# Opening of an encoder trunk: first weights by halves, matmuls of ones, held-back second-half work, another order of early pairs

## Chip, cores and metric

One core of a Trainium2 chip. The metric is the time of one execution on the device, in microseconds; the median of the runs counts. "PE" is TensorE (matmuls), "DVE" VectorE, "ACT" ScalarE, "POOL" GpSimd, "SP" the engine that issues nearly all transfers.

## The reference

Two request groups (512 and 256 tokens, 1024 wide) pass through the same trunk. Everything is float32.

```python
def swiglu(h, wg, wu, wd):
    return (jax.nn.silu(h @ wg) * (h @ wu)) @ wd

def even_layer(x, ...):                       # layer 0
    x = x + 0.5 * swiglu(rmsnorm(x, f1_n), f1_g, f1_u, f1_d)
    x = x + mixer_ab(rmsnorm(x, mix_n), ...)  # gated mixing beside windowed attention
    x = x + 0.5 * swiglu(rmsnorm(x, f2_n), f2_g, f2_u, f2_d)
    return x

def odd_layer(x, ...):                        # layer 1
    x = x + 0.5 * swiglu(rmsnorm(x, f1_n), f1_g, f1_u, f1_d)
    x = x + mixer_c(rmsnorm(x, mix_n), ...)   # neighbourhood attention
    x = x + 0.5 * swiglu(rmsnorm(x, f2_n), f2_g, f2_u, f2_d)
    return x
```

After both layers comes a last rmsnorm. The inner width of swiglu is 2816. The change touches only the swiglu blocks and the norms ahead of them.

## The kernel before

**Phases.** Six follow one another: l0f1, l0m, l0f2, l1f1, l1m, l1f2 (swiglu blocks have an f, mixers an m). x lies in the core as eight tiles of 128 channels by 768 tokens and stays there. The tokens are worked in two halves of 384 (half 0, half 1).

**A float32 product in three.** An operand is split into a rounded part (`whi`, or a name ending in h, made on ACT) and the rest (`wlo`, or a name ending in l, made on DVE). A product of two operands takes three matmuls: high with high, high with low, low with high.

**A block by seven products.** A swiglu block works on pairs of 256 inner columns, 11 of them. Each pair's gate and up matrices are seen as 2 by 2 blocks (channels 0 to 511 and 512 to 1023, two tiles of 128 columns), as are the token halves and channel halves of x. Seven block products per matrix take the place of eight. The operands on the side of x are b11 and b21 (half 0, split directly), and t1, t2, t3, n4, b22, which need half 1; `self.made` lists those that are there. One block product is 12 matmuls of 384 columns (four channel tiles, three each).

**Early pairs.** The first four pairs (`EARLY`) begin with the two products that need half 0 only: `p1` (weights times b11, for gate and up) and `p2` (weights times b21, added into the same PSUM bank). Between them the result of `p1` is copied out (line 524), and `p2` must wait for that copy. When 1/rms of half 0 is there, `hidden(0, 0)` scales both sums and multiplies silu(gate) by up (lines 508 to 511); this frees the two banks. `ORDER` lists, by hand, the order in which the stages p1, p2 and hidden of the four early pairs are issued. Their later five products (t2, t3, n4, t1, b22) follow pair by pair. Banks come from two rings of four, `mm` and `aux`; line 481 chooses.

**1/rms beside the products.** The norm does not hold up the products: x is multiplied by its gain only, and 1/rms is applied in `hidden`. Squares are made on ACT and added on DVE (`norm_add`). `norm_tok` sums them over channels by matmuls with a column of ones and computes 1/rms in small DVE steps (`rsqrt`, lines 265 to 276), `norm_spread` makes two diagonal matrices (`diag`, DVE line 256 and ACT line 254) and spreads them over the channels by two matmuls with ones.

**Who orders what.** PE's instructions run in the order in which the program issues them. On the other engines a scheduler orders them by priority, which follows the program's order unless raised (`high_priority`); every engine then runs its own queue in order. Side work (norms, operands of half 1) lives in generators: each yields a delay, and `tick` resumes those that are due on a model clock `self.t`, which counts the matmuls issued so far (0.16 for one of 384 columns). `run_until` resumes them at once where a result is needed. So the delays (`DELAY0`, `DELAY1`: ahead of the row sum, and between it and the spread) place norm matmuls between the products in PE's queue.

**The opening.** `build` makes the constants, loads x half 0 in eight transfers with the first four weight tiles (512 KB each: gate and up of pairs 0 and 1) between them, then x half 1. `second()` makes what needs half 1 (`feed`, then squares and sums); its instructions on ACT follow the second copy of `p1` (`issue_after`).

**Other blocks.** l1f1 follows another block, so its operands of half 1 are made as the block before ends. l0f2 and l1f2 follow a mixer: `self.unfed` is not empty there, and `behind` makes the operands.

## Time and profile before

| what | us |
|---|---|
| median of 3 runs | 2620.62 |
| lowest, highest | 2618.2, 2620.9 |
| profiled execution, its own time | 2616.48 |
| its span in the profile | 2614.7 |
| PE busy in the span | 2553.1 |
| DVE busy | 2264.1 |
| ACT busy | 1366.3 |

The span is what the profiler recorded of the profiled execution; that execution's own time is 1.8 us more. The median of the other runs is 4.1 us above the profiled one. Busy shares are means over six phases and say little of one stage, so the views are read by stretches and by single rows. In a timeline row the first number is the start, the second the duration, and brackets hold the time for which the engine idled before and what ended that.

### The profile page before, as it was taken

Reading aid. Unit: us, or ns where it says so; the run is one execution under the profiler, and the core shown is the slowest. Engines: PE = TensorE matmul, PEld = TensorE weight load, DVE = VectorE, ACT = ScalarE, POOL = GpSimd, SP = SyncE. Lnnn points to the kernel's source line nnn. Section 1 sums busy time; section 2 is a strip of 40 time slices with the busy share of each in tenths; the row PEclk is TensorE's granted clock in tenths of the full one; section 3 lists DMA queues with packets and bytes.
Section 4 is the critical chain, followed back from the end, with each engine's and each line's share of the span. In section 5 each row is a group of like instructions: output and inputs, shape, how many; then the busy total and the mean of one; then the engine's idle time right before and its main releaser. Section 6 shows DMA issues by size and latency. Waiting matters only on the chain.

```text
span 2614.7 us, 41195 instructions
## 1 busy us (share of the span) xinstructions
PE 2553.1 (98%) x15094; PEld 2488.8 (95%) x15094; DVE 2264.1 (87%) x4793; ACT 1366.3 (52%) x2851; POOL 88.4 (3%) x172
## 2 busy tenths in 40 slices
PE   7999999998999999999999999999999999999997
PEld 7999999987899999999999999989898999999997
DVE  8998899889779989889999888986677699988897
ACT  7544454555655545445654445454445475444543
POOL 0000000000100000000000000001222100000000
PEclk9999999999999999999999999999999999999999
DMA  5333222421223322222322222232221332222221
GB/s 172 112 112 95 81 65 65 160 73 45 82 77 97 97 65 81 66 81 81 97 81 81 74 72 73 72 129 63 63 64 40 106 99 88 81 73 73 73 69 69
DMA packets 83898, 218.99 MB, mean 84 GB/s; under 512 B 20080, under 2 KB 32880, under 8 KB 83696
## 3 DMA queue, kind: packets, MB, share of 16 engines
q1 hardware_dynamic: 83552, 216.34, 26.3%
q8 instruction: 118, 1.93, 0.3%
q14 instruction: 84, 0.69, 0.1%
q10 hardware_dynamic: 144, 0.03, 0.0%
HBM read 206.90 MB, written 15.07 MB: 85 GB/s over the span
## 4 chain that ended last, share of the span: by engine, by line
PE 88%; DVE 8%; ACT 2%; issue 1%; DMA 1%; SPq 0%; DVEq 0%; ACTq 0%
PE ps_mm L140 55%; PE ps_aux L140 32%; DVE wlo L115 1%; PE ps_aux L144 1%; DMA raw<-in_w 1%; DVE xl L741 1%; ACT p L913 1%; DVE p L922 0%; DVE p L907 0%; DVE tl L197 0%; DVE tmp L362 0%; ACT xh L740 0%; DVE x L708 0%; DVE ol L197 0%; ACT whi L114 0%
## 5 line engine op out<-in xcount | busy, mean ns | idle before, releaser
L114 ACT CAST whi<-s 128x512 fp32r<-128x512 f32 x496 | 305.1, 620 | 413.7 <-DVE s L611 169.9
L114 ACT CAST whi<-raw 128x512 fp32r<-128x512 f32 x512 | 311.4, 618 | 232.5 <-PE ps_mm L140 98.7
L115 DVE TENSOR_TENSOR wlo<-s,whi 128x512 fp32r<-128x512 f32 x496 | 337.4, 686 | 56.3 <-ACT whi L114 53.9
L115 DVE TENSOR_TENSOR wlo<-raw,whi 128x512 fp32r<-128x512 f32 x494 | 337.7, 691 | 24.9 <-ACT whi L114 20.7
L140 PE MATMUL ps_mm<-db,whi 128*128 128x384 f32 x864 | 219.3, 334 | 0.4 <-DVE sg L508 0.4
L140 PE MATMUL ps_aux<-dt,whi 128*128 128x384 f32 x864 | 219.1, 334 | 0.0
L140 PEld LDWEIGHTS ps_mm<-db,whi 128*128 128x128 f32 x864 | 155.9, 188 | 0.7 <-DVE sg L508 0.7
L140 PEld LDWEIGHTS ps_aux<-dt,whi 128*128 128x128 f32 x864 | 156.0, 188 | 0.0
L140 PE MATMUL ps_mm<-xh,whi 128*128 128x512 f32 (+1 forms) x416 | 147.3, 354 | 3.6 <-ACT xh L740 3.6
L140 PE MATMUL ps_mm<-db,wlo 128*128 128x384 f32 x432 | 144.3, 334 | 0.0
L140 PE MATMUL ps_aux<-dt,wlo 128*128 128x384 f32 x432 | 144.3, 334 | 0.0
L140 PE MATMUL ps_mm<-xl,whi 128*128 128x512 f32 (+1 forms) x416 | 142.3, 342 | 1.1 <-DVE xl L741 1.1
L140 PE MATMUL ps_mm<-xh,wlo 128*128 128x512 f32 (+1 forms) x416 | 141.9, 341 | 0.0
L611 DVE TENSOR_TENSOR s<-raw,raw 128x512 f32<-128x512 f32 x124 | 84.0, 686 | 21.3 <-DMA raw<-in_w 21.1
L611 DVE TENSOR_TENSOR s<-raw 128x512 f32<-128x512 f32 x124 | 85.2, 687 | 18.6 <-DMA raw<-in_w 18.3
L499 DVE TENSOR_TENSOR u<-ps_aux,u 128x384 f32<-128x384 f32 x176 | 97.2, 552 | 4.0 <-PE ps_aux L140 3.9
L140 PE MATMUL ps_aux<-dh,whi 128*128 128x384 f32 x384 | 97.7, 335 | 0.6 <-DVE x L708 0.6
L913 ACT ACTIVATE p<-p,st 128x256 f32<-128x256 f32 (+3 forms) x144 | 68.9, 480 | 54.5 <-DVE st L911 54.4
L663 DVE TENSOR_TENSOR x<-ps_aux,x 128x384 f32<-128x384 f32 x160 | 84.9, 552 | 13.0 <-PE ps_aux L140 13.0
L140 PEld LDWEIGHTS ps_mm<-xh,whi 128*128 128x128 f32 x416 | 79.9, 192 | 13.9 <-ACT xh L740 4.7
L140 PE MATMUL ps_mm<-oh,whi 128*128 128x384 f32 x256 | 88.7, 346 | 4.6 <-DVE x L890 4.0
L663 DVE TENSOR_TENSOR x<-ps_mm,x 128x384 f32<-128x384 f32 x160 | 86.2, 551 | 5.8 <-PE ps_mm L140 5.4
(486 smaller groups left out, 8046.3 us busy)
## 6 DMA issues: line engine op xcount, KB each, us to landing
raw<-in_w SPq DMA_DIRECT2D x350, 512.0 KB, 3.7
xdm<-x SPq DMA_DIRECT2D x16, 384.0 KB, 2.3
x<-in_x SPq DMA_DIRECT2D x16, 192.0 KB, 5.4
x<-xdm SPq DMA_DIRECT2D x8, 384.0 KB, 3.3
xold<-xdm SPq DMA_DIRECT2D x8, 384.0 KB, 3.0
out_y<-y SPq DMA_DIRECT2D x8, 384.0 KB, 2.4
tab<-skew SPq DMA_DIRECT2D x8, 256.0 KB, 5.6
raw<-in_w SPq DMA_DIRECT2D x8, 256.0 KB, 2.6
```

Source lines behind the costliest of these rows:

```text
L114: nc.scalar.copy(hi, src)
L115: (eng or nc.gpsimd).tensor_tensor(out=lo, in0=src, in1=hi.bitcast(F32), op=ALU.subtract)
L140: self.nc.tensor.matmul(out, lhsT=lhsT, rhs=rhs, start=start, stop=stop, **kw)
L144: self.nc.tensor.transpose(out, src, self.ident)
L499: nc.vector.tensor_tensor(out=t, in0=bank[key, n], in1=t, op=ALU.add)
L611: f = lambda o, x, y, op: self.nc.vector.tensor_tensor(out=o, in0=x, in1=y, op=op)
L663: nc.vector.tensor_tensor(out=o, in0=ps, in1=o, op=ALU.add)
L741: nc.vector.scalar_tensor_tensor(out=lo, in0=src, scalar=gain, in1=hi.bitcast(F32), op0=ALU.mult, op1=ALU.subtract)
L913: nc.scalar.activation(outs[i], outs[i], AF.Exp, bias=nm[:, i : i + 1], accum_out=sm[:, i : i + 1])
```

## The change

- The first four weight tiles are loaded as eight halves of 256 KB: the channel half that `p1` needs first, then the other. The very first half goes through ACT's queue, the others through SP's, three between x's first and second four tiles and four behind those.
- The constant of ones is made before the identity; a copy on ACT of part of it stands at the start, so ACT's table load comes there.
- 22 matmuls of ones by ones (`WARM`) are issued on PE ahead of the first product. Their result is not used.
- The split of the first four weight halves is placed in ACT's queue behind the 1st, 4th, 5th and 6th square (`HOLD`).
- `second()` is held until six copies of `p1` exist and the first 1/rms has been issued; its ACT instructions follow the sixth copy, its DVE instructions the last piece of the first `diag`.
- `diag` is issued together with the row sum and `rsqrt`, and no longer at the time of the spread.
- Delays: the opening has its own for half 0 (`DELAYS`) and half 1 (`DELAYT`); `DELAY0` elsewhere goes from (7.0, 11.0) to (7.0, 13.0).
- Where no mixer precedes (l0f1 and l1f1; `mixed` is false) the early pairs go in another order, and pair 2 instead of pair 3 takes its banks from `aux`. Blocks behind mixers keep theirs.
- In the opening, b21 weights of pairs 0 and 1 lose the raised priority, and `hidden(0, 0)` of those pairs gains it.
- The transfers of the bias tables (`self.spare`) start four units later, since the eight halves count as eight units and the four tiles counted as four.

```diff
-DELAY0 = (7.0, 11.0)
+DELAY0 = (7.0, 13.0)
+DELAYS = (11.6, 8.5)
+WARM = 22
+HOLD = (0, 3, 4, 5)
 DELAY1 = (26.0, 12.0)
+DELAYT = (22.0, 12.0)
-ORDER = (0, 1, 0, 1, 0, 2, 1, 3, 2, 3, 2, 3)
+ORDERS = (0, 1, 0, 1, 2, 2, 0, 1, 3, 2, 3, 3), (0, 1, 0, 1, 0, 2, 1, 3, 2, 3, 2, 3)
...
     def norm_spread(self, y, pool=None):
 
-        nc = self.nc
+        return self.spread(self.diags(y, pool))
+
+    def spread(self, diags):
+
+        rb = self.psum(self.aux, "aux")
+        for i, diag in enumerate(diags):
+            self.mmul(rb[:, :H], self.onesr, diag, i == 0, i == 1)
+        return rb[:, :H]
...
-            self.mmul(rb[:, :H], self.onesr, diag, i == 0, i == 1)
-        return rb[:, :H]
+            res.append(diag)
+        self.rooted.append(last.ins)
+        return res
...
         with self.tc.high_priority():
-            y = self.norm_tok(self.acc, c0, c1)
+            diags = self.diags(self.norm_tok(self.acc, c0, c1))
         yield d1
         with self.tc.high_priority():
-            self.r[h] = self.norm_spread(y)
+            self.r[h] = self.spread(diags)
...
         for n in (1, 2):
-            while len(self.copied) < 2:
+            while len(self.copied) < 6 or not self.rooted:
                 yield 0.2
-            with self.tc.issue_after(self.copied[1]):
+            with self.tc.issue_after(self.copied[5]), self.tc.issue_after(self.rooted[0]):
...
-        yield from self.norm_half(h, *(DELAY1 if h else DELAY0))
+        yield from self.norm_half(h, *((DELAY1 if len(self.rooted) > 1 else DELAYT) if h else DELAY0 if self.rooted else DELAYS))
...
+        mixed = bool(self.unfed)
...
+            fresh = bool(self.first)
...
-                    mm = key == "Y" or key == "X" and p != EARLY - 1
+                    mm = key == "Y" or key == "X" and p != EARLY - (1 if mixed else 2)
...
-                with self.tc.high_priority() if early and (b in ("b11", "b21") or b == "t2" and p == EARLY - 1) else nullcontext():
+                with ExitStack() as stack:
+                    if fresh and b == "b11":
+                        stack.enter_context(self.tc.issue_after(self.squares[HOLD[len(self.copied)]]))
+                    if early and (b == "b11" or b == "b21" and not fresh or b == "t2" and p == EARLY - 1):
+                        stack.enter_context(self.tc.high_priority())
                     st = self.wsplit(w, nc.vector)
...
-                hidden(0, 0, bank["X", "gate"], bank["X", "up"])
+                with self.tc.high_priority() if fresh else nullcontext():
+                    hidden(0, 0, bank["X", "gate"], bank["X", "up"])
...
-        for p in ORDER:
+        for p in ORDERS[mixed]:
...
+            def first(i, k, eng=None):
+                name = pre + ("gate", "up")[i % 2]
+                self.raw(name, 4 * k, 4, i // 2 * 2 * P, P, raws[i][:, k * 512 : k * 512 + 512], eng)
+
+            first(0, 0, nc.scalar)
+        nc.gpsimd.memset(self.ones, 1.0)
+        nc.vector.tensor_copy(self.onesr, self.ones)
+        nc.scalar.copy(space, self.ones[:, :96])
+        make_identity(nc, self.ident)
...
+        if kind == "f":
+            ps = self.psum(self.aux, "aux")
+            for _ in range(WARM):
+                nc.tensor.matmul(ps[:, :P], lhsT=self.onesr, rhs=self.onesr, start=True, stop=True)
...
                 if h == 0 and m % 4 == 3 and kind == "f":
-                    pre = f"{self.phases[0][:2]}_ffn{self.phases[0][3]}"
-                    self.first += [self.raw(f"{pre}_w_{n}", 0, KD, m // 4 * 2 * P, P) for n in ("gate", "up")]
+                    for i in range(4):
+                        if m > 4 or i:
+                            first(i, m // 4)
```

More of the change, by code (lines that the diff above doesn't have):

```diff
@@ L97, in raw @@
         self.woff += size
-        raw = self.rawp.tile([P, nk * n], F32, tag="raw", name=f"raw{i}")
-        self.nc.sync.dma_start(raw, src)
-        if self.spare and i >= 16:
+        if raw is None:
+            raw = self.rawp.tile([P, nk * n], F32, tag="raw", name=f"raw{i}")
+        (eng or self.nc.sync).dma_start(raw, src)
+        if self.spare and i >= 20:
             self.spare.pop(0)()
@@ L1412, in build @@
         nc = self.nc
-        self.cp.tile([P, 96], F32, tag="space", name="space")
+        space = self.cp.tile([P, 96], F32, tag="space", name="space")
+        todo = [KIND[p] for p in self.phases] + [("last", 6)]
+        kind = todo[0][0]
         self.ident = self.cp.tile([P, P], F32, tag="ident", name="ident")
-        make_identity(nc, self.ident)
         self.ones = self.cp.tile([P, P], F32, tag="ones", name="ones")
-        nc.gpsimd.memset(self.ones, 1.0)
         self.onesr = self.cp.tile([P, P], F32R, tag="onesr", name="onesr")
-        nc.vector.tensor_copy(self.onesr, self.ones)
         self.gains = self.cp.tile([P, 64], F32, tag="gains", name="gains")[:, : KD * len(NORMS)]
         nc.scalar.dma_start(self.gains, self.aps["gains"])
+        if kind == "f":
+            pre = f"{self.phases[0][:2]}_ffn{self.phases[0][3]}_w_"
+            raws = [self.rawp.tile([P, KD * P], F32, tag="raw", name=f"first{i}") for i in range(4)]
+            self.first += [t.rearrange("p (k n) -> p k n", k=KD) for t in raws]
+            def first(i, k, eng=None):
[6 more added lines that the diff above has]
+        make_identity(nc, self.ident)
         self.ngains = self.cp.tile([P, 64], F32, tag="ngains", name="ngains")[:, : KD * len(NORMS)]
@@ L1424, in build @@
         self.x = [self.xp.tile([P, T], F32, tag=f"x{m}", name=f"x{m}") for m in range(KD)]
-        todo = [KIND[p] for p in self.phases] + [("last", 6)]
-        kind = todo[0][0]
         if kind == "f":
```

13 lines of the change are left out of this document (8 added, 5 removed).

## Prediction

> **What bounds the kernel now.** I read the page's head and chain first, then TensorE's waits over the span, then the opening by stretches and in order of time.
>
> ```profile
> span 2614.7 us, 41195 instructions
> PE 2553.1 (98%) x15094; PEld 2488.8 (95%) x15094; DVE 2264.1 (87%) x4793; ACT 1366.3 (52%) x2851; POOL 88.4 (3%) x172
> PE 88%; DVE 8%; ACT 2%; issue 1%; DMA 1%; SPq 0%; DVEq 0%; ACTq 0%
> ```
>
> PE sets the end nearly everywhere, and VectorE (DVE) is close behind it. So the change can only take what PE loses, and it must not run into DVE. What PE loses by cause, over the span (total, times, longest):
>
> ```profile
> PE ps_mm L140 <- ACT whi L114: 9.2, 1, 9.2
> PE ps_aux L140 <- DVE diag L256: 6.5, 4, 3.4
> PE ps_mm L140 <- DVE sg L508: 6.5, 3, 3.6
> PE ps_mm L140 <- ACT p L524: 5.5, 1, 5.5
> ```
>
> 9.2, 5.5 and the longest of the `sg` waits, 3.6, all lie in the opening. Stretches of it (PE, weight loads, DVE, ACT, POOL; then clock, DMA share, GB/s):
>
> ```profile
> 0.00:25.00 25.00, 15.60 (x78) 15.05 (x78) 17.53 (x41) 19.95 (x40) 1.28 (x8) 1.00 0.83 292
> 25.00:45.00 20.00, 11.15 (x43) 10.82 (x44) 19.98 (x48) 16.62 (x35) 0.00 (x0) 0.74 0.25 51
> 45.00:80.10 35.10, 35.10 (x207) 35.10 (x206) 31.34 (x71) 18.15 (x37) 0.00 (x0) 1.00 0.44 132
> 80.10:114.50 34.40, 34.40 (x200) 34.33 (x199) 34.17 (x64) 19.41 (x39) 0.00 (x0) 1.00 0.42 139
> ```
>
> PE has holes until 45 us and none after; DVE is full from 25 to 45 and again from 80 to 114.5. PE in order of time:
>
> ```profile
> 9.15 0.69 PE L140 MATMUL ps_mm<-b110h,whi 128*128 128x384 f32 x1 [9.15 <-ACT whi L114]
> 13.83 0.34 PE L140 MATMUL ps_mm<-b110h,wlo 128*128 128x384 f32 x1
> ...
> 19.75 0.72 PE L140 MATMUL ps_aux<-ones,acc 128*128 128x1 f32 x6
> ...
> 30.24 0.69 PE L140 MATMUL ps_mm<-b210h,whi 128*128 128x384 f32 x1 [5.49 <-ACT p L524]
> 31.68 0.53 PE L140 MATMUL ps_mm<-b211l,whi 128*128 128x384 f32 x1
> 32.00 0.53 PE L140 MATMUL ps_mm<-b211h,wlo 128*128 128x384 f32 x1
> 34.24 0.34 PE L140 MATMUL ps_mm<-b210h,whi 128*128 128x384 f32 x1
> ...
> 36.33 0.51 PE L140 MATMUL ps_aux<-diag,onesr 128*128 128x384 f32 x2
> 40.45 0.45 PE L140 MATMUL ps_mm<-b110h,whi 128*128 128x384 f32 x1 [3.61 <-DVE sg L508]
> ...
> 80.60 0.33 PE L140 MATMUL ps_mm<-t20h,whi 128*128 128x384 f32 x1
> ```
>
> The row at 80.60 is the first matmul of pair 1's late part; before it lie 26 products (16 of the four early pairs, 10 of pair 0) of 12 matmuls each. At full clock a matmul costs 34.40/200 = 0.172 us, a product 2.06, 26 of them 53.7; the two row sums and the two spreads add about 2.1, in all 55.8. PE took 80.60 - 9.15 = 71.45. So 15.7 us are lost behind the first matmul: 9.1 as waits, and most of the rest as half clock: after the 5.49 us of idling, matmuls stand 0.32 apart (31.68, 32.00) until 34.24, 4.0 us for 12 that need 2.06. The same is seen from 9.15 to 13.83 and after 40.45.
>
> Who made PE wait:
>
> ```profile
> 1.11 0.23 DVE L1419 CAST onesr<-ones 128x128 fp32r<-128x128 f32 x1 [1.11 <-POOL ones L1417]
> 3.35 1.28 ACT L354 ACT_TABLE_LOAD   x1 [3.35 <-DMA x<-in_x]
> 8.49 0.62 ACT L114 CAST whi<-raw 128x512 fp32r<-128x512 f32 x1 [1.39 <-DMA raw<-in_w]
> 20.51 0.16 DVE L265 TENSOR_SCALAR sm<-ps_aux 128x3 f32<-128x3 f32 x1 [0.59 <-PE ps_aux L140]
> 29.73 0.46 ACT L524 COPY p<-ps_mm 128x384 f32<-128x384 f32 x1
> 32.14 0.66 DVE L256 TENSOR_SCALAR diag<-ident,yh 128x128 fp32r<-128x128 f32 x3
> 39.86 0.54 DVE L508 TENSOR_TENSOR sg<-ps_mm,acc 128x384 f32<-128x384 f32 x1
> 55.90 0.16 DVE L265 TENSOR_SCALAR sm<-ps_aux 128x3 f32<-128x3 f32 x1
> 64.86 0.67 DVE L256 TENSOR_SCALAR diag<-ident,yh 128x128 fp32r<-128x128 f32 x3
> 116.19 0.56 DVE L499 TENSOR_TENSOR u<-ps_aux,u 128x384 f32<-128x384 f32 x1 [1.62 <-PE ps_aux L140]
> ```
>
> The first weights reach ACT only at 8.49. The copy of pair 1's first product, which PE needs before it may add to that bank, runs at 29.73, because second-half work stands ahead of it on ACT. The 1/rms chain of half 0 takes from 20.51 to 32.80 on DVE, and `sg`, which frees the bank for pair 2, runs at 39.86.
>
> **The change part by part.**
>
> *First weights by halves, table load early.* The table load (1.28) moves under the wait for x, so x is converted at best 1.28 earlier. The first weight half, 256 KB, now goes from ACT's queue beside x: at the 292 GB/s of the first stretch it takes 0.9 of the transfers. I take x's first conversion 0.4 earlier, at 4.3 (bounds 1.3 earlier, 0.1 later; both ends are between these rows). ACT then does one conversion, one square and the first `whi`, so the first product can start near 5.5. The Trainium skill (DMA: Bandwidth & Descriptors, "Issuing engines are not separate DMA queues") says that DMAs from different engines interleave on the same 16 DMA engines, so that a second issuer saves only issue time. By that rule the half costs x its full 0.9. No run here shows two issuers with large loads. SP issues three loads more before x's second half; nothing needs that half before 25 us.
>
> *Matmuls of ones.* 22 of them follow `onesr`, ready at 1.34. The trace has no 128x128 matmul: the six with one column take 0.72 together, 0.12 each, and a 384-column one at half clock 0.32. So 22 take 2.6 to 7.0 us and end between 4.0 and 8.4. I take 0.2, ending at 5.8, and the first real matmul at 6.0 (range 5.2 to 8.4) against 9.15. What they can save is the slow start of 9.15 to 13.83: 4.7 us for 14 matmuls that need 2.4, so 2.3. I count on half of it.
> The Trainium skill (TensorE: Matmul & The Clock Gate, "What's actually happening") says that full rate comes after about 3.4 us of sustained work in a window that runs freely. The wait at 30.24 followed by 4.0 us at half rate agrees with that. By its 107 ns for a cold 128-column matmul the burst would last 2.35 us, an estimate from that page, and would not lift the clock.
>
> *Second-half work behind six copies and the first diag.* This takes second-half conversions and squares out of ACT's queue ahead of the copies: the 5.5 wait and its half-clock time (4.0 - 2.06 = 1.9) go. Queued behind the new wait on DVE and ACT are t2, then the squares of half 1, then t3, n4, t1, b22. PE needs t2 at product 17.
>
> *Order 0 1 0 1 2 2 and pair 2 in the other banks; `hidden` of pair 0 first.* Pair 2 no longer needs a bank that waits for 1/rms, so PE has 12 products instead of 8 before it does. The 3.6 and its half-clock time (about 1.6, as after 30.24 but shorter) go. Banks of pair 2 stay taken until its own `hidden`; nobody asks for them before pair 0's fifth step.
>
> PE's side alone: 6.0 + 55.8 + 1.1 (half of the slow start) = 62.9 instead of 80.6, **17.7 saved**. But what is late next? *DVE.* It was busy 17.53 + 19.98 + 31.34 + 34.17 = 103.0 us by 114.5, and the same work must be done. At 116.19 it waits for PE again: it was ahead. Its cheap work was done in PE's holes:
>
> ```profile
> L115 DVE TENSOR_TENSOR wlo<-raw,whi 128x512 fp32r<-128x512 f32 x13 | 8.5, 683 | 0.2 <-ACT whi L114 0.2
> L220 DVE TENSOR_TENSOR acc<-acc,sq 128x384 f32<-128x384 f32 x13 | 7.1, 548 | 0.0
> L362 DVE SCALAR_TENSOR_TENSOR tmp<-x,gains,tmp 128x384 f32<-128x384 f32 x4 | 2.4, 603 | 0.0
> ```
>
> With second-half work held back DVE has, until the first diag, 8 low parts of x (0.6 each as the L362 group, 4.8), 7 adds (0.55: 3.8), 10 `wlo` (0.65: 6.5) and the chain of 16 small ones (0.16: 2.5) with diag 0.7: 18.3, of which some 10% overlap, so 16.5. When is diag? The row sum now stands in the seventh product: 6.0 + 6.2 x 2.06 + about 1 slow = 19.8. The chain took 12.3 when each link had another instruction behind it; its links alone are 2.5 + 0.7. I take 6, since the work that stood between is mostly held back: diag at 26 (bounds 23 and 33). So DVE idles (26 - 4.3) - 16.5 = 5.2. Then it is full: 4.3 + 5.2 + 103.0 = 112.5 against 114.5, 2.0 saved. To that comes what it had done ahead at 114.5 and may now do late: six sums and `wlo` for products not begun, 3.7, and operands not due before the down projection, up to 2.5. I take 5.0. **Opening: 7.0 saved** (0 if diag is at 33; 17.7 if DVE's load can be put off).
>
> *Later phases.* DELAY0 moves the first spread 2 model us later where the blocks follow others, and the diags are issued with the chain. Two of the four diag waits lie at such places:
>
> ```profile
> 778.77 0.67 PE L140 MATMUL ps_aux<-diag,onesr 128*128 128x384 f32 x2 [1.22 <-DVE diag L256]
> 1262.20 0.62 PE L140 MATMUL ps_aux<-diag,onesr 128*128 128x384 f32 x2 [1.38 <-DVE diag L256]
> ```
>
> 1.22 + 1.38 = 2.6; 2 us later covers each. The changed order also applies at 1262; it moves DVE's work there by four products, for between -1 and +1, taken as 0. The other two are at the end, where the chain is serial, and stay.
>
> Sum: 7.0 + 2.6 = **9.6 us**. The profiled execution took 2616.48 (span 2614.7), so 2606.9; the runs shown have a median of 2620.62, on which it is **2611.0**.
>
> **The rivals.**
>
> *PE's holes close fully.* DVE's work is put off without PE noticing: from 114.5 on DVE has slack, as the wait at 116.19 shows. 17.7 + 2.6 = 20.3: 2600.3. Against it: 34.17 of 34.40 busy from 80 to 114.5.
>
> *The first product stays slow.* If the burst doesn't lift the clock, PE's side is 1.1 worse. Where DVE sets the pace this changes nothing: 2611.0; with the rival above, 2601.4. After 9.15 PE worked 4.7 us before it was fast, and half of the burst's range (2.6 to 7.0) is shorter: chance 0.5 that it is so, within each case. The rule of the Trainium skill's page on the clock gate, above, speaks for it.
>
> *The gain is given back.* The chain on DVE is as long as before, 12.3, so diag is at 33 and DVE idles 7 us more: opening 0, later 2.6: 2618.0, no change.
>
> *The second 1/rms becomes the wait (slower).* By the model's clock the row sum of half 1 now falls at the end of product 22, and the spread is forced after product 24: 4.2 us of PE between them. Before, DELAY1 put 12 model us between them, and the chain with its diag took from 55.90 to 65.53, 9.6. PE then waits 9.6 - 4.2 = 5.4, and as after 30.24 runs at half clock for 1.9 more: 7.3. My forecast has it inside the time in which PE waits for DVE anyway. It decides if that time is used up earlier, by diag at 33 and PE idling ahead of t2, and the later diag waits stay: 7.3 - 0.5 = 6.8 slower, 2627.4.
>
> **How the numbers follow.** No change means within 0.2%, 5.2 us, about what a measurement can tell. Forecast, 2611.0: 0.50. Holes closed, 2600 to 2602: 0.19. Given back, 2618: 0.17. Slower, 2627: 0.14. The first two make 0.69 faster; a small part of the given-back case (diag between 26 and 33) adds 0.01. Range: from 2600 to 2619, which leaves out the slower case and little more.
>
> **What would show it.** Right: the first matmul near 6; the copies of pairs 0 to 2 each right behind their products; no `p` wait and no `sg` wait in the opening; diag near 26; DVE without idling from there to over 100 us, PE waiting instead for `t2`, `t3` or the second diag; pair 1's first t2 matmul near 70; no diag wait near 770 and 1250. Wrong: diag after 33, a PE wait of over 5 us at the second spread with the clock at half behind it, or the first matmul after 8.4.

## The result and the profile after

The changed kernel is slower by 0.29%.

| | before | after |
|---|---|---|
| median of 16 runs, us | 2618.27 | 2625.92 |
| lowest, us | 2616.62 | 2620.29 |
| ratio after/before, 95% interval | | 1.0029 (1.0022 to 1.0036) |
| profiled execution, its own time, us | 2616.48 | 2623.09 |
| its span, us | 2614.7 | 2621.3 |

One of the 16 runs of before took 3152.41 us and is left out of the ratio. The forecast was 2611.0, with a range of 2600 to 2619. The two profiled executions differ by 6.6 us, so the profile of after contains what has to be explained. Its head and the longest of TensorE's waits over the span (total, times, longest):

```profile
span 2621.3 us, 41230 instructions
PE 2561.4 (98%) x15116; PEld 2495.2 (95%) x15116; DVE 2266.1 (86%) x4793; ACT 1365.8 (52%) x2852; POOL 87.8 (3%) x172
...
PE ps_mm L146 <- DVE sg L532: 11.8, 3, 6.9
PE ps_aux L146 <- DVE diag L273: 7.4, 3, 3.4
...
PE ps_mm L146 <- DVE wlo L121: 3.0, 4, 1.6
```

The 9.2 for the first weights and the 5.5 for `p` are gone, as forecast. But `sg` has grown from 6.5 to 11.8, its longest from 3.6 to 6.9. The opening in the same four stretches as before (PE, weight loads, DVE, ACT, POOL; then clock, DMA share, GB/s):

```profile
0.00:25.00 25.00, 23.64 (x123) 23.13 (x124) 16.62 (x35) 17.22 (x34) 1.19 (x8) 1.00 0.83 297
25.00:45.00 20.00, 13.12 (x65) 12.80 (x65) 16.73 (x40) 18.04 (x39) 0.00 (x0) 0.78 0.51 131
45.00:80.10 35.10, 27.78 (x143) 26.26 (x142) 32.66 (x76) 17.35 (x37) 0.00 (x0) 0.93 0.26 83
80.10:114.50 34.40, 34.40 (x189) 34.13 (x189) 33.54 (x63) 19.25 (x39) 0.00 (x0) 0.95 0.32 97
```

The first stretch now holds 123 matmuls instead of 78 (22 of them ones). The second has 65 for 43. The loss is in the third: 143 matmuls instead of 207. DVE, which was full from 25 to 45 (19.98 of 20), has holes there now (16.73). PE in order of time:

```profile
1.25 4.96 PE L1473 MATMUL ps_aux<-onesr 128*128 128x128 f32 x22 [1.25 <-DVE onesr L1457]
6.00 0.63 PE L146 MATMUL ps_mm<-b110h,whi 128*128 128x384 f32 x1
...
9.48 0.34 PE L146 MATMUL ps_mm<-b110h,whi 128*128 128x384 f32 x1
...
30.38 0.51 PE L146 MATMUL ps_aux<-diag,onesr 128*128 128x384 f32 x2
...
40.89 0.69 PE L146 MATMUL ps_mm<-b110h,whi 128*128 128x384 f32 x1 [6.88 <-DVE sg L532]
...
54.00 0.44 PE L146 MATMUL ps_mm<-t20h,wlo 128*128 128x384 f32 x1 [1.63 <-DVE wlo L121]
57.85 0.44 PE L146 MATMUL ps_mm<-t20h,whi 128*128 128x384 f32 x1 [1.84 <-ACT whi L120]
...
79.04 0.87 PE L146 MATMUL ps_aux<-diag,onesr 128*128 128x384 f32 x2 [3.44 <-DVE diag L273]
...
80.67 0.53 PE L146 MATMUL ps_aux<-b221h,wlo 128*128 128x384 f32 x1
80.99 0.53 PE L146 MATMUL ps_aux<-b222h,whi 128*128 128x384 f32 x1
...
85.48 0.33 PE L146 MATMUL ps_mm<-t20h,whi 128*128 128x384 f32 x1
```

PE starts its products 3.15 us earlier (6.00 for 9.15) and reaches pair 1's first t2 matmul 4.88 us later (85.48 for 80.60). After the wait of 6.88 and again after that of 3.44, matmuls stand 0.32 apart, which is half clock. Behind the first matmul PE waits 14.2 us up to 85.48 (6.88, 1.63, 1.84, 0.41 at 58.87, 3.44), where before has 9.1. By the count of the prediction, 85.48 - 6.00 - 55.8 leaves 23.7 lost; by the distances of the rows, about 8 of the 9.5 that are not waits are half clock (6 of 6.6 in before). Why `sg` is late is seen on DVE (first five rows) and ACT (last two):

```profile
22.14 0.16 DVE L283 TENSOR_SCALAR sm<-ps_aux 128x3 f32<-128x3 f32 x1 [0.76 <-PE ps_aux L146]
...
27.01 0.67 DVE L273 TENSOR_SCALAR diag<-ident,yh 128x128 fp32r<-128x128 f32 x3
28.42 0.69 DVE L121 TENSOR_TENSOR wlo<-raw,whi 128x512 fp32r<-128x512 f32 x1 [0.74 <-ACT whi L120]
...
30.68 0.55 DVE L358 TENSOR_TENSOR tmp<-x 128x384 f32<-128x384 f32 x1
...
40.29 0.55 DVE L532 TENSOR_TENSOR sg<-ps_mm,acc 128x384 f32<-128x384 f32 x1
...
30.31 0.62 ACT L360 ACTIVATE tmp<-x,gains 128x384 f32<-128x384 f32 x1
...
34.34 0.46 ACT L432 COPY acc<-ps_aux 128x384 f32<-128x384 f32 x1
```

DVE's part of the first diag is done at 27.7, and PE has spread 1/rms by 30.9. But at 30.3 the held second-half work is let go on ACT, right behind the sixth copy of `p1` (29.94), and at 30.7 on DVE. It stands ahead of the copy of the spread 1/rms (ACT, 34.34), and on DVE from 30.68 to 40.29 ahead of `sg`, which frees the banks that pair 3 needs.

Past the opening, the start of each phase is seen by its row sums. Before (first five) and after:

```profile
515.99 1.39 PE L140 MATMUL ps_aux<-ones,acc 128*128 128x1 f32 x12
765.79 0.72 PE L140 MATMUL ps_aux<-ones,acc 128*128 128x1 f32 x6
799.06 0.72 PE L140 MATMUL ps_aux<-ones,acc 128*128 128x1 f32 x6
1249.06 0.72 PE L140 MATMUL ps_aux<-ones,acc 128*128 128x1 f32 x6
1288.66 0.72 PE L140 MATMUL ps_aux<-ones,acc 128*128 128x1 f32 x6
```

```profile
522.84 1.39 PE L146 MATMUL ps_aux<-ones,acc 128*128 128x1 f32 x12
771.87 0.72 PE L146 MATMUL ps_aux<-ones,acc 128*128 128x1 f32 x6
807.63 0.72 PE L146 MATMUL ps_aux<-ones,acc 128*128 128x1 f32 x6
1257.17 0.72 PE L146 MATMUL ps_aux<-ones,acc 128*128 128x1 f32 x6
1295.11 0.72 PE L146 MATMUL ps_aux<-ones,acc 128*128 128x1 f32 x6
```

The opening and l0f1 cost 6.85 (522.84 - 515.99). That is 4.88 up to pair 1's t2, and another 2.0 between there and the first mixer, of it 1.2 in two waits near 129 us (0.31 for `whi`, 0.87 for `wlo`). Early l0f2 costs 2.5 (35.76 between its two row sums for 33.27), early l1f1 gains 1.66 (37.94 for 39.60). The rest of the span moves by about -1.

### The profile page after: what moved, and what is told of

It reads as the page before. It is cut to its first block, busy times and chain, and to the rows that moved or that the text cites. A ratio compares the mean times of both kernels' runs of the same rounds, so it can differ in the third digit from the quotient of the medians.

```text
span 2621.3 us, 41230 instructions
## 1 busy us (share of the span) xinstructions
PE 2561.4 (98%) x15116; PEld 2495.2 (95%) x15116; DVE 2266.1 (86%) x4793; ACT 1365.8 (52%) x2852; POOL 87.8 (3%) x172
## 4 chain that ended last, share of the span: by engine, by line
PE 89%; DVE 7%; ACT 3%; issue 1%; DMA 0%; DVEq 0%; ACTq 0%; POOL 0%; POOLq 0%
PE ps_mm L146 55%; PE ps_aux L146 33%; PE ps_aux L150 1%; DVE wlo L121 1%; DVE xl L766 1%; ACT p L938 1%; DVE p L947 0%; DMA raw<-in_w 0%; DVE p L932 0%; DVE tl L203 0%; ACT sq L225 0%; ACT whi L120 0%; DVE s L636 0%; ACT xh L765 0%; DVE ol L203 0%
## 5 line engine op out<-in xcount | busy, mean ns | idle before, releaser
L121 DVE TENSOR_TENSOR wlo<-raw,whi 128x512 fp32r<-128x512 f32 x486 | 332.0, 691 | 28.4 <-ACT whi L120 24.5
```

The costliest lines, as they stand in the source:

```text
L121: (eng or nc.gpsimd).tensor_tensor(out=lo, in0=src, in1=hi.bitcast(F32), op=ALU.subtract)
```

## The experiments

Two theories of the 6.85:

- **Q, place in the queue.** The held work is let go too early or in the wrong place: it stands ahead of the scale copy and of `sg`. Let it go behind them, and PE's gain comes through.
- **C, what DVE can do.** DVE has a fixed amount of work ahead of pair 1's late part. While half 1 is held back DVE has too little to do, and that time is not made up. Whichever wait of PE is removed, the lost time returns as another one.

A third question was which of the other edits (first loads, ones, order, delays) matter at all. One table serves all runs. P1 is the start of pair 1's first t2 matmul; DVE's busy time is that from 4 us to P1, idle the rest of that stretch; "15 to 30" is DVE's busy time in that stretch of 15 us.

| kernel | P1 | DVE busy | DVE idle | 15 to 30 | first mixer row sum | time, median | ratio to before (95%) |
|---|---|---|---|---|---|---|---|
| before | 80.60 | 69.13 | 7.5 | 14.21 | 515.99 | | |
| after | 85.48 | 70.80 | 10.7 | 9.75 | 522.84 | 2625.92 | 1.0029 (1.0022 to 1.0036) |
| e1_behind_hidden | 84.54 | 70.32 | 10.2 | 10.30 | 524.34 | 2626.08 | 1.0037 (1.0025 to 1.0050) |
| e2_no_hold | 80.44 | 70.77 | 5.7 | 14.05 | 515.83 | 2618.06 | 1.0001 (0.9992 to 1.0010) |
| e3_old_order | 79.60 | 69.99 | 5.6 | 11.85 | 514.96 | 2618.84 | 1.0005 (0.9996 to 1.0014) |
| e5_hold_fourth_copy | 77.63 | 68.11 | 5.5 | 14.69 | 515.06 | 2617.43 | 0.9995 (0.9985 to 1.0005) |
| e6_adds_on_pool | 86.29 | 74.27 | 8.0 | 9.84 | 521.65 | 2628.5 | 1.0034 (1.0020 to 1.0047) |
| e7_first_loads_only | 81.47 | 69.07 | 8.4 | 13.16 | 517.13 | 2618.07 | 1.0000 (0.9991 to 1.0009) |
| e8_delay0_11 | 87.78 | 71.19 | 12.6 | 10.34 | 525.11 | 2624.05 | 1.0022 (1.0013 to 1.0031) |
| e9_fourth_copy_and_diag | 81.16 | 69.40 | 7.8 | 11.70 | 516.79 | 2620.45 | 1.0007 (0.9998 to 1.0016) |
| e10_fourth_copy_delay11 | 78.17 | 68.37 | 5.8 | 14.74 | 515.59 | 2614.6 | 0.9986 (0.9977 to 0.9995) |
| e11_no_ones | 76.39 | 68.00 | 4.4 | 14.83 | 513.78 | 2615.96 | 0.9989 (0.9980 to 0.9998) |
| e12_later_phases_only | 80.34 | 69.03 | 7.3 | 14.30 | 515.92 | 2618.13 | 0.9999 (0.9990 to 1.0007) |

Each ratio is against runs of before on the same chip; their medians were 2617.6 to 2618.62. e4 has the opening of before and is left out of the table. The busy and idle time come from the rows by stretches, of which these are the stretch from 15 to 30 and the sum up to P1, for before and after:

```profile
15.00:30.00 15.00, 9.75 (x59) 9.43 (x57) 14.21 (x40) 14.66 (x31) 0.00 (x0) 0.91 0.67 206
...
sum 76.60, PE 62.35 PEld 61.47 DVE 69.13 ACT 54.43 POOL 0.00; mean PE 15.59 PEld 15.37 DVE 17.28 ACT 13.61 POOL 0.00
```

```profile
15.00:30.00 15.00, 14.89 (x88) 14.52 (x87) 9.75 (x30) 7.95 (x18) 0.00 (x0) 1.00 0.68 241
...
sum 81.48, PE 67.16 PEld 64.81 DVE 70.80 ACT 52.84 POOL 0.00; mean PE 16.79 PEld 16.20 DVE 17.70 ACT 13.21 POOL 0.00
```

In after, PE is full from 15 to 30 (14.89) and DVE does 9.75; before had it nearly the other way round. That P1 is 4 us plus DVE's busy and idle time is only a way of writing it. What the runs add is that the busy part stays between 68.0 and 71.2 in every kernel but e6, while the idle part goes from 4.4 to 12.6 and P1 with it. They do not tell DVE from ACT: ACT's busy time from 15 to 30 moves the same way (14.66 before, 7.95 after, 13.87 in e2, 14.21 in e5). A third theory, that ACT's lost time is what costs, has no run of its own.

**e1: the held work behind the first `hidden`.**

```diff
-            while len(self.copied) < 6 or not self.rooted:
+            while len(self.copied) < 6 or len(self.hid) < 2:
                 yield 0.2
-            with self.tc.issue_after(self.copied[5]), self.tc.issue_after(self.rooted[0]):
+            with self.tc.issue_after(self.copied[5]), self.tc.issue_after(self.hid[1]):
...
-                nc.vector.tensor_tensor(out=v, in0=u, in1=r, op=ALU.mult)
+                self.hid.append(nc.vector.tensor_tensor(out=v, in0=u, in1=r, op=ALU.mult).ins)
```

> The changed kernel, with second-half work on DVE held behind the four multiplications by 1/rms of pairs 0 and 1 instead of behind the first diag. Theory Q (place in the queue): the 6.9 us wait for sg comes from some twenty second-half instructions that stand ahead of sg on DVE although 1/rms is there. Then sg runs at 32 to 33 instead of 40.3, the wait shrinks to under 1.5 with no half clock behind it, and pair 1's first t2 matmul comes at 76 to 78 instead of 85.5; time 7 to 9 below the changed kernel. Rival C (capacity of DVE): the same work is only done later; the wait moves to the t2 and t3 products, pair 1 begins at 83 to 86, time within 3 us of the changed kernel.

In order of time, DVE's `sg` and then PE:

```profile
32.49 0.55 DVE L533 TENSOR_TENSOR sg<-ps_mm,acc 128x384 f32<-128x384 f32 x1
...
44.06 0.69 PE L147 MATMUL ps_mm<-b210h,whi 128*128 128x384 f32 x1 [5.41 <-ACT p L549]
```

`sg` runs 7.8 us earlier than in after (32.49 for 40.29), and its wait is gone. P1 moves by 0.94 (84.54 for 85.48), and the time not measurably (2626.08). A wait of 5.41 for `p` stands at 44.06 instead, and the second spread waits 4.59 (3.44 in after). Q is right about what made `sg` late and wrong about the time.

**e2: the held work let go at the second copy, as before.**

```diff
-            while len(self.copied) < 6 or not self.rooted:
+            while len(self.copied) < 2:
                 yield 0.2
-            with self.tc.issue_after(self.copied[5]), self.tc.issue_after(self.rooted[0]):
+            with self.tc.issue_after(self.copied[1]):
```

> The changed kernel with the hold undone: second-half work follows the second copy only, as before the change; loads, matmuls of ones, order and delays stay. Theory Q: the copies of p1 and the 1/rms chain fall behind second-half work again, p wait of 4 to 6 us, chain of 10 to 12 us, but the sg wait of 6.9 shrinks to under 4; pair 1 begins near 80; time 4 to 6 below the changed kernel. Rival C: DVE no longer idles ahead of the first diag (5 us) and gets through its work earlier; pair 1 begins near 76, time 8 to 10 below the changed kernel.

```profile
21.84 0.69 PE L146 MATMUL ps_mm<-b110h,whi 128*128 128x384 f32 x1 [7.18 <-ACT whi L120]
```

The loss is gone: 515.83 at the first mixer row sum, ratio 1.0001. So the hold is what makes after slow. PE's wait of 6.88 at 40.89 has given way to one of 7.18 at 21.84, as long, yet P1 is 5.0 us earlier: where PE waits isn't what it costs. DVE works 14.05 of the 15 us from 15 to 30. Everything else in the change, together, is worth nothing here that can be measured. The run does not choose between the theories: P1 is where Q had put it (near 80) and not at C's 76, the `p` wait that Q expected did not come, and the time, 0.28% below that of after in the ratios or about 7.3 us, lies between the two.

**e3: the old order and banks, with the hold at the fourth copy and the first diag.**

```diff
-ORDERS = (0, 1, 0, 1, 2, 2, 0, 1, 3, 2, 3, 3), (0, 1, 0, 1, 0, 2, 1, 3, 2, 3, 2, 3)
+ORDERS = (0, 1, 0, 1, 0, 2, 1, 3, 2, 3, 2, 3), (0, 1, 0, 1, 0, 2, 1, 3, 2, 3, 2, 3)
...
-            while len(self.copied) < 6 or not self.rooted:
+            while len(self.copied) < 4 or not self.rooted:
...
-                    mm = key == "Y" or key == "X" and p != EARLY - (1 if mixed else 2)
+                    mm = key == "Y" or key == "X" and p != EARLY - 1
```

> The changed kernel with the old order and banks of the early pairs (0 1 0 1 0 2 1 3 2 3 2 3), and the hold behind the fourth copy, since the fifth and sixth now come behind the first hidden. Theory Q: PE has only 8 products before it needs the bank, so it waits longer, 7 to 12 us around 24 to 36; pair 1 begins at 85 to 90, time equal to the changed kernel or up to 4 above. A rival, that the new order itself makes the loss by its banks: the wait shrinks below 4, and time falls by 4 or more.

```profile
37.42 0.69 PE L146 MATMUL ps_mm<-b110h,whi 128*128 128x384 f32 x1 [10.05 <-DVE sg L532]
```

PE waits 10.05 here, where after has 6.88, and yet P1 (79.60) is 1.0 us earlier than before and 5.9 earlier than in after. The wait is as long as Q expected, P1 is not at its 85 to 90; the rival's short wait did not come either. With the old order the fifth and sixth copies come behind the first `hidden`, so the hold had to go to the fourth copy: the run moves two things, and e9 separates them.

**e4: the transfers of the bias tables four units later.**

```diff
-        if self.spare and i >= 16:
+        if self.spare and i >= 20:
```

> The kernel before with only the new first part: halves, early table load, matmuls of ones. No hold, old order, old delays. Theory Q: the first matmul comes at 6 instead of 9.15 and runs at full clock from about 9, but the copies of pair 1 stand where they stood on ACT, so the p wait grows from 5.5 to 8 or more; pair 1 begins at 79 to 80.6; time 0 to 1.5 below the kernel before. Rival C: DVE and ACT start 1 to 2 us earlier and all behind them moves along; time 2 to 5 below the kernel before.

This run was meant to be the change's first part, but its edit left out the split loads and the matmuls of ones: the build remained that of before, and only the shift of the bias tables was in it. What the expectation says was therefore not measured here; e7 does it. The time was 2617.45, ratio 1.0000 (0.9991 to 1.0010), so that shift alone does nothing measurable. It also shows how far an opening with no other change moves between executions: first matmul at 8.57 for 9.15, P1 at 80.09 for 80.60.

**e5: the held work let go at the fourth copy, not behind the diag.**

```diff
-            while len(self.copied) < 6 or not self.rooted:
+            while len(self.copied) < 4:
                 yield 0.2
-            with self.tc.issue_after(self.copied[5]), self.tc.issue_after(self.rooted[0]):
+            with self.tc.issue_after(self.copied[3]):
```

> The changed kernel with second-half work released at the fourth copy of p1 instead of the sixth, and not held behind the first diag; new order kept. Capacity theory C, as the first runs bear it out (DVE does 69 to 71 us of work before pair 1 in every kernel, and pair 1 begins that much plus DVE's idle time after 4 us): DVE idles less between 15 and 30, by 2 to 4 us, so pair 1 begins at 81 to 83 instead of 85.5 whatever PE then waits for; time 2 to 4 below the changed kernel. Queue theory Q: the sg wait stays, since second-half work stands ahead of sg even more; pair 1 at 85 or later, time as the changed kernel.

```profile
37.24 0.69 PE L146 MATMUL ps_aux<-b210h,whi 128*128 128x384 f32 x1 [5.75 <-ACT p L548]
```

DVE is full from 15 to 30 (14.69), P1 is at 77.63, 7.9 us before that of after and 3.0 before that of before. C gave the direction but too little (81 to 83); Q, which kept the `sg` wait, is wrong. At the first mixer row sum 0.9 of the 3.0 is left: from P1 to there it took 437.43, before 435.39. The time is that of before (0.9995). In its last block PE waits 3.5 us for `u` (DVE, 1.96 and 1.58), more than the 0.9 that was left; before has no such wait there.

**e6: seven adds of half 1's squares on POOL.** If DVE's load is the bound, taking 3.9 us off it should show.

```diff
-                        self.norm_add(m, H, T)
+                        self.norm_add(m, H, T, self.nc.gpsimd)
...
-            nc.vector.tensor_tensor(out=self.acc[:, a:b], in0=self.acc[:, a:b], in1=sq, op=ALU.add)
+            (eng or nc.vector).tensor_tensor(out=self.acc[:, a:b], in0=self.acc[:, a:b], in1=sq, op=ALU.add)
```

> The changed kernel with the seven additions of half 1's squares in the opening (DVE, 0.55 us each, 3.9 in all) moved to POOL, which idles there; one takes about 1 us on POOL. Nothing else changes. Theory C: pair 1 begins 2 to 4 us earlier, at 81.5 to 83.5, DVE's busy time before it falls to 67; time 2 to 4 below the changed kernel. Theory Q: the additions aren't what PE waits for; pair 1 begins within 1 us of 85.5 and time stays.

The same groups on DVE from 30 to 45 us in after (first two rows) and in e6, with POOL's adds (busy, mean ns of one, idle before):

```profile
L380 DVE SCALAR_TENSOR_TENSOR tmp<-tmp,ngains 128x384 f32<-128x384 f32 x4 | 2.4, 611 | 0.0
...
L358 DVE TENSOR_TENSOR tmp<-x 128x384 f32<-128x384 f32 x4 | 2.2, 552 | 0.0
```

```profile
L380 DVE SCALAR_TENSOR_TENSOR tmp<-tmp,ngains 128x384 f32<-128x384 f32 x4 | 3.9, 982 | 0.1
L358 DVE TENSOR_TENSOR tmp<-x 128x384 f32<-128x384 f32 x4 | 3.0, 750 | 0.0
...
L226 POOL TENSOR_TENSOR acc<-acc,sq 128x384 f32<-128x384 f32 x7 | 8.8, 1252 | 31.2 <-ACT sq L225 30.8
```

The edit didn't unload DVE. It took 3.9 us of adds off it and made it 3.5 us busier (74.27 for 70.80), because DVE's own instructions took 1.4 to 1.6 times as long, in the mean of these groups, while POOL ran. So it does not tell whether a lighter DVE would be faster. It does tell something about a heavier one: with 3.5 us more of DVE's work P1 moved by 0.8 only, less than the 2.3 that lie between two executions of one opening (after and e8), and DVE's idle time fell from 10.7 to 8.0. So DVE had room for more work in after, which speaks against C in its strict form. Why the instructions grew longer is told below.

**e7: the first part alone** (before, with the loads by halves, the table load early and the 22 matmuls of ones; order, hold and delays of before).

```diff
+WARM = 22
...
+            first(0, 0, nc.scalar)
...
+        nc.scalar.copy(space, self.ones[:, :96])
...
+            for _ in range(WARM):
+                nc.tensor.matmul(ps[:, :P], lhsT=self.onesr, rhs=self.onesr, start=True, stop=True)
```

> The kernel before with the new first part alone: halves, early table load, matmuls of ones (and the later start of the bias-table transfers). Theory C: PE starts at 6 instead of 9.15, but DVE starts only 1 us earlier; pair 1 begins 0 to 1.5 us earlier, at 79 to 80.6, and the waits for p and sg grow by about what the start gained; time 0 to 1.5 below the kernel before. A rival, that the start is worth what PE gains: pair 1 at 76 to 77.5, time 3 to 5 below.

PE in e7, and below it the start of the fifth product in before:

```profile
14.77 0.52 PE L142 MATMUL ps_mm<-b113l,whi 128*128 128x384 f32 x1
15.09 0.40 PE L142 MATMUL ps_mm<-b113h,wlo 128*128 128x384 f32 x1
...
20.61 0.42 PE L142 MATMUL ps_mm<-b210h,whi 128*128 128x384 f32 x1
```

```profile
20.34 0.42 PE L140 MATMUL ps_mm<-b210h,whi 128*128 128x384 f32 x1
```

The first product starts at 6.00, 3.15 earlier than before, and nothing comes of it: P1 81.47, time 2618.07, ratio 1.0000. The lead is gone before any long wait: matmuls still stand 0.32 apart at 15.1, where before they did so until 13.83, and the fifth product starts at 20.61, 0.27 later than before. C had the waits grow by what the start gained. They did not: PE waits 3.70 for `p` at 28.74, 1.13 for the diag at 36.40, 3.51 for `sg` at 40.36, in all no more than the 9.1 of before. So this run shows that the early start alone, spent at half clock, was worth nothing; whether a lead that lasts would be lost to DVE it does not test.

**e8: `DELAY0` back at 11, all else as in after.**

```diff
-DELAY0 = (7.0, 13.0)
+DELAY0 = (7.0, 11.0)
```

> The changed kernel with DELAY0 at (7.0, 11.0) as before. If the later spread is what costs in l0f2 (a wait of 2.3 us for sg with half clock behind it, in place of a diag wait of 1.2) and in l1f2, then both fall back: no sg wait near 790, diag waits of 1.2 near 780 and 1.4 near 1265 return, time 0 to 3 below the changed kernel. If the cost there comes from something else, the sg wait stays and time rises by the 1.4.

Between the two row sums of l0f2 stand 33.64 us (807.63 - 773.99) instead of 35.76. The diag waits 0.62 there again and ACT's part 0.32, but the `sg` wait is 0.17 instead of 2.27. l1f1 keeps its 37.94 and has no diag wait. In e3, with the old order there and the delay at 13, it is 37.94 too. So neither the delay nor the order is needed for that gain; what the runs share is the early issue of the diag. The time, 2624.05, is 1.9 below that of after, with intervals that overlap. This execution's opening, with the same code as after's, reached P1 2.3 us later.

**e9: the fourth copy and the first diag** (after with 6 copies replaced by 4, the wait for the diag kept).

```diff
-            while len(self.copied) < 6 or not self.rooted:
+            while len(self.copied) < 4 or not self.rooted:
                 yield 0.2
-            with self.tc.issue_after(self.copied[5]), self.tc.issue_after(self.rooted[0]):
+            with self.tc.issue_after(self.copied[3]), self.tc.issue_after(self.rooted[0]):
```

> The changed kernel with the hold on ACT behind the fourth copy, but DVE's second-half work still behind the first diag. It tells which of the two holds costs. If it is the diag: DVE idles 5 us between 15 and 30 as in the changed kernel, pair 1 begins at 83 or later, time within 3 us of the changed kernel. If it is the copies: DVE idles about 1 us there, pair 1 begins near 77.6, time 7 to 9 below the changed kernel, as with both released. Theory C: in both cases pair 1 begins 4 us plus DVE's work (68 to 71) plus DVE's idle time.

P1 81.16, time 2620.45, ratio 1.0007: between after and e5 in all columns, so neither case of the expectation alone. Four copies for six gives back 4.3 of P1, dropping the diag another 3.5, and DVE's busy time from 15 to 30 goes 9.75, 11.70, 14.69. In P1 both halves of the hold cost. In the time only the first step is clear of noise: the intervals of e9 and e5 overlap. With the same hold, the old order (e3, 79.60) is 1.6 ahead of the new one at P1, which is no more than the 2.3 between after and e8, whose openings have the same code.

**e10: e5 with `DELAY0` at 11**, the version that the runs so far pointed to.

```diff
-DELAY0 = (7.0, 13.0)
+DELAY0 = (7.0, 11.0)
...
-            while len(self.copied) < 6 or not self.rooted:
+            while len(self.copied) < 4:
...
-            with self.tc.issue_after(self.copied[5]), self.tc.issue_after(self.rooted[0]):
+            with self.tc.issue_after(self.copied[3]):
```

> Second-half work released at the fourth copy, not behind diag, and DELAY0 back at (7.0, 11.0). Theory C with the finding on DELAY0: opening as with the fourth copy alone (row sum of the first mixer at 515), the sg wait of 2.3 near 786 gone, no waits for u (L523) in l1f2, the gain of 1.7 in l1f1 kept: time 2612 to 2616, 2 to 6 below the kernel before. If the waits in l1f2 don't hang on DELAY0, time stays at 2617 to 2618.

2614.6, ratio 0.9986 (0.9977 to 0.9995): faster than before by 0.14%, and than after by 0.43% in the two ratios. Its ratio is the lowest of this study. 0.14% is below what was called a measurable difference above, yet the interval excludes 1, and that of e11 does too. It overlaps that of e5, so the time does not show what `DELAY0` adds. In the profile the `sg` wait in l0f2 is 0.17 for 2.26 in e5, and the 3.5 us of waits for `u` in the last block have shrunk to 0.17.

**e11: e10 without the matmuls of ones.**

```diff
-WARM = 22
+WARM = 0
```

> As the run with the fourth copy and DELAY0 at 11, without the 22 matmuls of ones. PE starts its first product near 5.5 at half clock and loses about 2 us until 10. Theory C: DVE sets the time of pair 1, so it begins within 1 us of the kernel with them; time within 1 us. Rival: the slow start is paid, pair 1 begins 2 us later and time is 2 us higher.

2615.96, ratio 0.9989 (0.9980 to 0.9998): not told apart from e10. P1 is 1.8 earlier (76.39 for 78.17), where both expectations had it the same or later; that is less than the 2.3 between after and e8. The first product starts at 5.43 and runs at half clock until about 9.5; with the ones, after was fast from 8.9, but e2, with the same 22 ones and the same first product at 6.0, only from 10.6. The ones are worth nothing that these runs can show.

**e12: the change in the later phases alone** (before with the diag issued beside the row sum, the new order and banks in l1f1 only, `DELAY0` 11).

```diff
-            y = self.norm_tok(self.acc, c0, c1)
+            diags = self.diags(self.norm_tok(self.acc, c0, c1))
...
+        mixed = bool(self.unfed) or bool(self.first)
...
-                    mm = key == "Y" or key == "X" and p != EARLY - 1
+                    mm = key == "Y" or key == "X" and p != EARLY - (1 if mixed else 2)
...
-        for p in ORDER:
+        for p in ORDERS[mixed]:
```

> The kernel before with the part for the later blocks alone: diag issued together with the row sum, DELAY0 at 11, the new order and banks in l1f1 only; the opening keeps its order, loads and delays. The diag waits of 1.2 near 778 and 1.4 near 1262 shrink to under 1 and 0.3; l1f1 gains 1.7 to 2.8, l0f2 stays within 0.5, the opening within 1: time 1.5 to 3.5 below the kernel before. If those gains come from DELAY0 at 13 or not at all: within 0.5 of the kernel before.

In the profile the 1.66 in l1f1 is there (37.94 for 39.60). In the time it isn't: 2618.13, ratio 0.9999. A gain of 1.7 us is 0.06%, inside the interval, and the executions of one kernel lie further apart than that.

## Why the prediction was wrong

The likeliest case failed, and with it the sign. Its steps in order:

- **First matmul at 6.0: right** (6.00). The first product took 3.48 us instead of 2.06, a loss of 1.4 where 1.1 was counted. The rival in which the burst doesn't lift the clock was right about the burst: 22 took 4.96 us, 0.225 each, and it ended at 6.21 with the clock still at half. The Trainium skill (TensorE: Matmul & The Clock Gate, "What's actually happening") has a window of 3413 ns that runs freely. The half clock from about 80.5 to 83.9 us in after, with matmuls 0.32 apart, lasts about that long, and the different end of the slow start in after (8.9) and e2 (10.6) fits a window that doesn't start with the kernel; the half clock from 40.89 to past 46 is longer. The Trainium skill's 107 ns for a cold 128-column matmul gave an estimate of 2.35 us for the burst, half of what was measured. By e7 the earlier start alone, and by e11 the ones, moved the time by nothing that shows. In e7 the lead was lost at half clock, so it does not say what a lead would be worth.
- **`p` wait gone, copies right behind their products: right** (each within 1 us).
- **Diag at 26: near** (27.0 to 27.7), the chain 5.5 us for the 6 forecast. So "the gain is given back", which needed diag at 33, was not the case that occurred.
- **"Then it is full": the step that failed.** The forecast let DVE idle 5.2 us from 4.3 to the diag and not at all after it. The first was near: 18.75 busy of 23.40 up to 27.7, so 4.7 idle. But from 27.7 to 45 it idled another 3.0 (14.29 of 17.30), and from 45 to P1 2.8 (37.68 of 40.48). Of these 5.8 us, 3.9 ended with something from ACT (`whi` at 28.42 and 30.07, `sg` at 43.30 and 44.12, the scale copy at 80.47) and 1.6 with PE. The forecast had only DVE as the next limit and no wait of DVE for ACT. It also let the hold end with the diag, though the held work waits for the sixth copy too: by its own terms that follows the tenth product, 6.0 + 10 x 2.06 + 1 + 0.7 = 28.3, and not 26. It ran at 29.94.
- **Lead of 5.0: not there.** It was to be work that DVE can put off. It can be read at the matmul that before starts at 114.61 (`t11l` by `whi`) and after at 119.70:

```profile
0.00:114.61 114.61, 96.36 (x525) 95.41 (x526) 103.10 (x221) 74.23 (x150) 1.28 (x8) 0.96 0.49 155
```

```profile
0.00:119.70 119.70, 104.13 (x546) 101.51 (x547) 103.28 (x219) 73.55 (x150) 1.19 (x8) 0.93 0.47 151
```

DVE had done 103.1 there in before and 103.3 in after; the least of any run is 101.4 (e11). So nothing was put off in after, and at most 1.7 elsewhere. At this matmul after is 5.1 late where it was to be 7.0 early. Of the 12.1 between, 6.9 are DVE's idle time (16.4 for the forecast's 9.5, start included) and 5.2 are work (the lead of 5.0 and 0.2 more). PE's holes closing fully, the rival on the fast side, fails by the same rows.
- **`sg` wait gone through the new order: wrong.** The forecast said that `hidden` goes first and did not ask what stands ahead of it in DVE's queue. Released at 30.3, four us before the scale copy, the held work had 9.6 us of DVE's queue ahead of `sg`. The text named the instructions queued behind the new wait; the error was to name those and not the ones that they in turn delay. e1 shows that mending this brings nothing.
- **The second 1/rms becomes the wait: the rival that came nearest,** with 0.14. It priced a wait of 5.4 and 1.9 of half clock; measured were 3.44 at 79.04 and 3.4 us of half clock, worth 1.7. Its time, 2627.4, is 1.5 from the measured one, and that is luck: its condition, diag at 33, didn't occur, the wait with its half clock came to 5.1 (3.44 + 1.7) where it priced 7.3, and the 0.5 that it took off has no row behind it. e2 and e5 have no wait there: that wait too comes from the hold.
- **Later phases, -2.6: half right.** At l1f1 the 1.38 is gone and 1.66 was gained, without the delay (e8) and without the order (e3). At l0f2 the 1.22 is gone, but `DELAY0` at 13 put `sg` 2.27 late, and the stretch is 2.5 longer. The forecast gave the delay the wait's worth and no price. A later spread makes what uses it later, and in l0f2 nothing stood between. The price was not the same each time. The rows at the wait in after and e5:

```profile
794.05 0.69 PE L146 MATMUL ps_mm<-b110h,whi 128*128 128x384 f32 x1 [2.27 <-DVE sg L532]
```

```profile
786.04 0.44 PE L146 MATMUL ps_mm<-b110h,whi 128*128 128x384 f32 x1 [2.26 <-DVE sg L532]
```

Behind the first, matmuls stand 0.32 apart until 797.1; behind the second 0.17 at once. With 13 the stretch took 35.76 to 35.82 in after, e3, e6 and e9, but 34.23 or 34.24 in e1, e2 and e5. With 11 it took 33.64, 33.65 and 33.65 (e8, e10, e12), and before 33.27. So the delay costs 0.6, and 1.5 more where half clock follows; 0.4 stays without it.

What is shown is that the hold makes after slow: undone, alone (e2) or in part (e5, e9), the time comes back. Why it costs is in part argued. For C speak that a wait of PE's that was taken away came back at another place (e1, e2, e5), and that P1 went with DVE's idle time and not with the length of PE's longest wait (e2, e3). But C's forecasts of P1 missed in e2 (76 for 80.44) and e5 (81 to 83 for 77.63), e6 speaks against its strict form, and PE's own account goes with P1 nearly as well: the start of the first product and all of PE's waits behind it make 18.3 before, 20.2 in after, 19.7 in e1, 17.2 in e2, 17.8 in e3 and 14.9 in e5. C wasn't shown by making DVE's work smaller, since e6 made it larger; moving adds to ACT, which is busy 52.84 of the 81.48 us in after, wasn't tried. Nor was ACT's share tried: in after it is busy 16.91 of the 17.30 us from 27.7 to 45. It also isn't settled why after's DVE does 1.7 us more before P1 than before's, nor where e10's 0.14% comes from. In its profile the row sums are 0.4 (first mixer) to 3.7 us (last mixer) ahead of before, yet its span is 2615.1 for 2614.7: l1m and l1f2 took longer there, and one trace of each kernel does not tell whether that is the code or the execution.

## What to carry to other kernels

Where a second engine is nearly as full as the bound one, a hole of the bound engine is when the second one gets ahead. Taking away a wait of 6.88 us moved P1 by 0.94 here (e1), and holding work back to shorten a queue cost what the other engines then idled. Before taking a wait out, add up busy and idle time of every engine that feeds the bound one, from the start to the first point where the bound one is full again, and ask of each edit whether it shrinks or grows the idle part; here DVE's and ACT's moved together, so neither may be left out of the count. When work is released later, check by the forecast's own times which of its conditions comes last, list what the work will stand ahead of at the new place on every queue, and price both the wait and the half clock behind it.

## What the hardware showed that was not expected

While POOL added 128x384 tiles (1252 ns each), DVE's instructions, all with two tile operands there, slowed down: L380 from 611 to 982 ns in the mean, single ones up to 1344 where 552 is usual, though POOL and DVE worked on different tiles. The Trainium skill (SBUF — State Buffer, "SBUF: two separate sides") describes a port pair that DVE, with two SBUF inputs, and GpSimd take in turn for a whole instruction, the other being blocked. A DVE instruction of 611 that waits out part of a POOL instruction of 1252 agrees with that.

Waits of a few us can cost more than they last. After the wait of 6.88 PE ran at half clock until past 46, after the one of 3.44 for 3.4 us, worth another 1.7. Smaller waits can do it too, but do not always: behind 1.84 and 0.41 at 57.85 and 58.87, matmuls stood 0.32 apart from 60.3 to 63.2, and behind the wait of 2.26 in l0f2 they did in some kernels and not in others. The clock column of the stretches does not show the slow start: before has 1.00 there from 0 to 25, with matmuls 0.32 apart until 13.83, so the starts of the rows have to be read. The runs of after lie between 2620 and 2632 us; the granted clock, as a mean over the span, was 0.991 in the three quickest and 0.988 in the four slowest (2629.9 to 2632.03).
